# Two 128x512 products of a recurrence move from GpSimd to VectorE

## The chip, the cores and the metric

The kernel runs on one core of one Trainium2 chip. It computes one layer of a decoder trunk for 512 tokens. The metric is device time in microseconds (us). Three runs of the kernel before took 846.41, 846.49 and 846.69 us; their median is 846.49 us.

A core has a matrix engine (TensorE, PE in the profile; its weight loads are listed as PEld), a vector engine (VectorE, DVE), an activation engine (ScalarE, ACT), a general engine (GpSimd, POOL), and a queue that issues most transfers (SyncE, SP). Each engine takes its own instructions strictly in the order in which the kernel issued them to it. They wait for one another through semaphores.

## The reference, cut to what matters

The layer is a half-step feed-forward block, a token mixer, and a second half-step feed-forward block. The change lies in the mixer. There a gated linear recurrence on 512 channels stands beside a sliding-window attention with 8 heads:

```python
r = jax.nn.sigmoid(block_diag(xc, w_rg, b_rg))
i = jax.nn.sigmoid(block_diag(xc, w_ig, b_ig))
log_a = LRU_C * r * jax.nn.log_sigmoid(lam)
a = jnp.exp(log_a)
mult = jnp.sqrt(-jnp.expm1(2.0 * log_a))
u = mult * (i * xc)                       # "inputs with their roots"
h = scan(h[t] = a[t] * h[t-1] + u[t])
y_lru = h * jax.nn.gelu(gate_lru)
p = softmax over (band of scores, sink)   # per block of 128 queries
y = concat(rms_norm(y_lru), rms_norm(p @ v)) @ w_o
```

The change concerns the product `mult * (i * xc)`.

## The kernel before, in words

Activations lie with channels on the 128 partitions and the 512 tokens along the free axis. The 512 recurrence channels are therefore four chunks, `ci` 0 to 3, each a 128x512 float32 tile. `us_[ci]` holds `i * xc` (in the profile this tile is named `xc`), `th[ci]` holds what becomes the root, and `rs_[ci]` the decay `a` (named `r`).

The order of all instructions is written out by hand; no planner moves anything. The mixer's middle part is a loop over `now` from 0 to 9 (line 1706). It drives eight attention units, `units[0]` to `units[7]`: four blocks of 128 queries (`b`) times two key/value groups (`n`). Each unit passes through four steps, spread over three turns of the loop:

- `scores` (lines 1618 to 1632): PE's score products for a block, issued once per block; then on DVE the mask (`COPY_PREDICATED`), a maximum (`TENSOR_REDUCE`), the negated maximum `nm` (L1630) and the sink's exponent `es` (L1632).
- `exps` (lines 1641 to 1645): four exponentials on ACT, which need `nm`; then the denominators on POOL (`den`, L1645).
- `turn_p`, one turn later (lines 1653 to 1660): PE transposes the probabilities (`pt`, L1653), ACT copies them out (`pa`, L1655), and POOL makes the part of the previous block (`pp`, L1659) and of the current one (`pa`, L1660) with two affine selects.
- `values`, two turns later (lines 1672 to 1680): PE multiplies with the values (`po`; L1672 needs `pp`, L1673 needs `pa`), and after every second unit DVE normalises (`yn`, L1680).

Between these steps `pump` issues pieces of the gate's projection on PE (`gt`, lines 498 to 500, three matmuls a piece), so that PE has work while the other engines prepare its next operands. `PUMPS` says how many pieces stand at each place. PE runs through this list in order too: if a transpose or a value product is not ready, the gate pieces behind it wait.

The recurrence is woven into the same loop. In turn 5 ACT takes the four square roots (L1573). In turn 6, behind unit 6's `scores` and other DVE work, stand the four products `root_u` (L1576) and the scans of chunks 2 and 3 (L1581). Unit 7's `scores` are behind those on DVE. On POOL, `root_u` stands behind unit 5's affine selects and unit 6's `den`, and ahead of unit 6's affine selects. Chunk 0's scan follows in turn 8 and chunk 1's behind the loop; a deferred split of an output weight (L184) follows chunk 0's scan on DVE. Behind the loop 5 pieces of the gate's projection are left for PE, then the transposes `atp` (L1751), then the output projection `wo` (L1794 and on).

## Time and profile before

| what | value |
|---|---|
| median of three runs | 846.49 us (846.41 to 846.69) |
| the profiled execution's own time | 847.31 us |
| its span, first to last instruction | 845.6 us |
| PE busy | 835.3 us, 99% of the span |
| DVE busy | 734.1 us, 87% |
| ACT busy | 525.1 us, 62% |
| POOL busy | 202.1 us, 24% |
| mean granted TensorE clock | 0.999 |

The timeline's columns are start (us from the span's start), duration in us, engine, line, operation, tiles as out<-in, shapes, and the count of instructions merged into the row. Brackets at the end give the engine's idle time in front of the row and what ended it. The duration of a row counts from when the instruction is issued to its engine, so it contains time in which it is held up there. Neighbouring instructions of one engine overlap by a little under 0.1 us, so the next row's start tells when an engine is free again. In the view of waits each row names who waited for whom, with the total in us, the count, and the longest single wait.

### The profile page before, as it was taken

Reading aid. Unit: us, or ns where it says so; the run is one execution under the profiler, and the core shown is the slowest. Engines: PE = TensorE matmul, PEld = TensorE weight load, DVE = VectorE, ACT = ScalarE, POOL = GpSimd, SP = SyncE. Lnnn points to the kernel's source line nnn. Section 1 sums busy time; section 2 is a strip of 40 time slices with the busy share of each in tenths; the row PEclk is TensorE's granted clock in tenths of the full one; section 3 lists DMA queues with packets and bytes.
Section 4 is the critical chain, followed back from the end, with each engine's and each line's share of the span. In section 5 each row is a group of like instructions: output and inputs, shape, how many; then the busy total and the mean of one; then the engine's idle time right before and its main releaser. Section 6 shows DMA issues by size and latency. Waiting matters only on the chain.

```text
span 845.6 us, 12586 instructions
## 1 busy us (share of the span) xinstructions
PE 835.3 (99%) x4568; PEld 725.1 (86%) x4568; DVE 734.1 (87%) x1020; ACT 525.1 (62%) x875; POOL 202.1 (24%) x213
## 2 busy tenths in 40 slices
PE   9999999999999999999999999999999999999996
PEld 9988888988988998998788899888788888888885
DVE  4978999988979865889989589799998998998996
ACT  6746756676666655556888447436657767666562
POOL 2023000230320334334456055112004114032001
PEclk9999999999999999999999999999999999999999
DMA  7249419397594899231311130167639939769742
GB/s 250 76 141 348 158 47 320 84 246 251 140 253 169 178 274 322 74 101 50 101 50 51 50 121 31 50 167 190 231 110 230 319 89 250 256 152 259 297 138 101
DMA packets 122767, 142.18 MB, mean 168 GB/s; under 512 B 23680, under 2 KB 81360, under 8 KB 122192
## 3 DMA queue, kind: packets, MB, share of 16 engines
q1 hardware_dynamic: 108576, 110.81, 40.8%
q0 software_dynamic: 13984, 30.42, 16.8%
q8 instruction: 36, 0.59, 0.3%
q14 instruction: 27, 0.22, 0.1%
q10 hardware_dynamic: 144, 0.13, 0.0%
HBM read 100.45 MB, written 40.89 MB: 167 GB/s over the span
## 4 chain that ended last, share of the span: by engine, by line
PE 89%; DVE 5%; DMA 2%; ACT 2%; issue 1%; POOL 1%; SPq 0%; DVEq 0%; ACTq 0%; POOLq 0%
PE aa L948 10%; PE ab L948 10%; PE da L948 5%; PE db L948 5%; PE yaa L1339 3%; PE bb L948 3%; PE ba L948 3%; PE yda L1339 2%; PE ya L498 2%; PE ya L499 2%; PE ya L500 2%; PE aa L878 1%; PE a_first L1198 1%; PE yab L1865 1%; PE yab L1863 1%; PE yab L1864 1%
## 5 line engine op out<-in xcount | busy, mean ns | idle before, releaser
L1108 POOL DMA_DIRECT2D yp_a<-stage x42 | 36.8, 1067 | 181.7 <-ACT stage L1105 160.9
L1108 POOL DMA_DIRECT2D yp_b<-stage x42 | 36.3, 1032 | 144.9 <-ACT stage L1105 121.6
L498 PE MATMUL ya<-hha,whi_ad 128*128 128x512 f32 x62 | 24.1, 389 | 0.0
L499 PE MATMUL ya<-hla,whi_ad 128*128 128x512 f32 x62 | 24.1, 389 | 0.0
L500 PE MATMUL ya<-hha,wlo_ad 128*128 128x512 f32 x62 | 24.1, 389 | 0.0
L681 POOL TENSOR_TENSOR acca_r<-acca_r,sq_r 128x512 f32<-128x512 f32 x6 | 8.0, 1326 | 45.4 <-ACT sq_r L529 45.4
L1977 POOL TENSOR_TENSOR last<-yp,grow 128x512 f32<-128x512 f32 x3 | 3.9, 1293 | 58.3 <-DVE yp L1972 58.3
L517 PE MATMUL an<-xh_mx,whi_xl 128*128 128x256 f32 x64 | 15.8, 287 | 0.0
L518 PE MATMUL an<-xh_mx,wlo_xl 128*128 128x256 f32 x64 | 15.5, 283 | 0.0
L1973 ACT ACTIVATE ysq<-yp 128x512 f32<-128x512 f32 (+1 forms) x9 | 5.3, 585 | 15.9 <-DVE yp L1972 15.7
L498 PE MATMUL gt<-xh_mx,whi_gt 128*128 128x512 f32 x32 | 14.2, 444 | 0.0
L500 PEld LDWEIGHTS ya<-hha,wlo_ad 128*128 128x128 f32 x62 | 11.6, 188 | 2.4
L1105 ACT COPY stage<-yab 128x512 f32<-128x512 f32 x12 | 6.5, 601 | 11.6 <-DMA yp_b<-stage 11.6
L498 PEld LDWEIGHTS ya<-hha,whi_ad 128*128 128x128 f32 x62 | 11.6, 188 | 2.4
L499 PEld LDWEIGHTS ya<-hla,whi_ad 128*128 128x128 f32 x62 | 11.6, 188 | 2.4
L529 ACT ACTIVATE sq_r<-yp_a 128x256 f32<-128x256 f32 (+1 forms) x10 | 5.0, 502 | 12.4 <-DVE yp_a L671 5.3
L498 PE MATMUL pub<-xh_f,whi_bu 128*128 128x512 f32 x32 | 12.6, 395 | 0.0
L500 PE MATMUL gt<-xh_mx,wlo_gt 128*128 128x512 f32 x32 | 12.6, 394 | 0.0
L498 PE MATMUL pgb<-xh_f,whi_bg 128*128 128x512 f32 x32 | 12.6, 393 | 0.0
L499 PE MATMUL gt<-xl_mx,whi_gt 128*128 128x512 f32 x32 | 12.6, 392 | 0.0
L498 PE MATMUL pq<-xh_mx,whi_q 128*128 128x512 f32 x32 | 12.5, 392 | 0.0
L573 ACT ACTIVATE xh_f<-xT,cols 128x256 fp32r<-128x256 f32 x16 | 8.1, 508 | 7.0 <-DVE xT L712 6.4
(2021 smaller groups left out, 3531.4 us busy)
## 6 DMA issues: line engine op xcount, KB each, us to landing
yp_a<-stage POOLq DMA_DIRECT2D x50, 256.0 KB, 8.9
yp_b<-stage POOLq DMA_DIRECT2D x50, 256.0 KB, 10.1
h_a<-za SPq DMA_DIRECT2D x16, 256.0 KB, 4.5
hxa<-h_a SPq DMA_DIRECT2D x16, 256.0 KB, 17.9
h_b<-zb SPq DMA_DIRECT2D x16, 256.0 KB, 3.7
hxb<-h_b SPq DMA_DIRECT2D x16, 256.0 KB, 18.8
xn<-in_x SPq DMA_DIRECT2D x8, 256.0 KB, 4.6
xT_hbm<-xT POOLq DMA_DIRECT2D x2, 1024.0 KB, 9.6
```

The lines of the kernel that those rows point to most:

```text
L498: pe.matmul(ps, hi[:, k, :], xh, start=start, stop=False)
L499: pe.matmul(ps, hi[:, k, :], xl, start=False, stop=False)
L500: pe.matmul(ps, lo[:, k, :], xh, start=False, stop=stop)
L517: pe.matmul(ps[:, sl], hi[:, k, :], xh, start=k == 0, stop=False)
L518: pe.matmul(ps[:, sl], lo[:, k, :], xh, start=False, stop=False)
L878: pe.matmul(o, w[:, k, js], x, start=first and i + j + k == 0, stop=k == 3 and i == 2, skip_group_check=True)
L948: pe.matmul(b[tb], x[:, blk], w[:, k, :], start=first and q + k + j == 0, stop=q + k == 2 and j == 2, skip_group_check=True)
L1108: pool.dma_start(o, st.rearrange("p (a b) -> p a b", a=2) if len(o.shape) == 3 else st, accum_op=ALU.add)
L1198: pe.matmul(banks[j][:, HALF[0]], ws[j][part][:, k, :], n1.xs[k][xpart][:, HALF[0]], start=k == 0 and part == xpart, stop=stop and k == KD ...
L1339: pe.matmul(o, a[:, k, ms], x[:, js], start=first and i + k + m % 2 == 0, stop=k == 1 and i == 2, skip_group_check=True)
L1863: pe.matmul(banks[i], hh[:, js], hi[:, k, :], start=first and k == 0, stop=False, skip_group_check=True)
L1864: pe.matmul(banks[i], hh[:, js], lo[:, k, :], start=False, stop=False, skip_group_check=True)
```

## The change

All four products are now issued to DVE. Chunks 0 and 1 were issued to POOL before. Nothing else is edited.

```diff
     def root_u(ci):
-        (pool if ci < 2 else dve).tensor_mul(us_[ci], us_[ci], th[ci])
+        dve.tensor_mul(us_[ci], us_[ci], th[ci])
```

The loop that calls it is unchanged, so on DVE the order becomes: products 0, 1, 2, 3, scans of chunks 2 and 3, then unit 7's scores. On POOL unit 6's affine selects follow directly behind its `den`. The scan of chunk 0 no longer waits for POOL. PE, ACT and SP have the same instructions in the same order; no transfer moves.

## The prediction

> **What bounds the kernel now.** I read the page's list of engines and its chain first. PE is busy all through, and the chain of work that ended last runs on PE for 89% of the span. A change elsewhere counts only where it makes PE wait, or ends a wait of PE.

> ```profile
> PE 835.3 (99%) x4568; PEld 725.1 (86%) x4568; DVE 734.1 (87%) x1020; ACT 525.1 (62%) x875; POOL 202.1 (24%) x213
> ...
> PE 89%; DVE 5%; DMA 2%; ACT 2%; issue 1%; POOL 1%; SPq 0%; DVEq 0%; ACTq 0%; POOLq 0%
> ```

> Next, the waits of PE alone. Apart from one at the start there are only these three:

> ```profile
> PE ab L948 <- ACT bb L953: 1.3, 1, 1.3
> PE yeb L1865 <- DVE hls L831: 0.3, 1, 0.3
> PE po L1673 <- POOL pa L1660: 0.3, 1, 0.3
> ```

> The last one is in our stretch: the value products of unit 6 wait for an affine select of POOL. So I read that stretch of the timeline engine by engine. POOL first:

> ```profile
> 441.67 1.47 POOL L1659 TENSOR_SCALAR_AFFINE_SELECT pp<-pa 128x512 f32<-128x512 f32 x1 [5.80 <-ACT pa L1655]
> 443.20 1.44 POOL L1660 TENSOR_SCALAR_AFFINE_SELECT pa<-pa 128x512 f32<-128x512 f32 x1
> 444.61 0.20 POOL L1645 TENSOR_TENSOR den<-dsum,es 128x4 f32<-128x4 f32 x1
> 444.76 2.51 POOL L1576 TENSOR_TENSOR xc<-xc,th 128x512 f32<-128x512 f32 x2
> 447.22 1.17 POOL L1659 TENSOR_SCALAR_AFFINE_SELECT pp<-pa 128x512 f32<-128x512 f32 x1
> 448.46 0.64 POOL L1660 TENSOR_SCALAR_AFFINE_SELECT pa<-pa 128x512 f32<-128x512 f32 x1
> 449.06 0.20 POOL L1645 TENSOR_TENSOR den<-dsum,es 128x4 f32<-128x4 f32 x1
> 449.21 0.64 POOL L1659 TENSOR_SCALAR_AFFINE_SELECT pp<-pa 128x512 f32<-128x512 f32 x1
> 449.91 1.44 POOL L1660 TENSOR_SCALAR_AFFINE_SELECT pa<-pa 128x512 f32<-128x512 f32 x1
> ```

> The two products occupy POOL from 444.76 to 447.27, and unit 6's selects (447.22, 448.46) stand behind them. An affine select takes 0.64 us alone and about 1.45 in company. DVE in the same stretch:

> ```profile
> 440.28 1.28 DVE L1576 TENSOR_TENSOR xc<-xc,th 128x512 f32<-128x512 f32 x2
> 441.48 2.72 DVE L1581 TENSOR_TENSOR_SCAN xc<-r,xc 128x512 f32<-128x512 f32 x2
> 444.13 0.40 DVE L1626 COPY_PREDICATED sc<-up,sc 128x256 f32<-128x256 uint8 x1
> ...
> 445.82 0.22 DVE L1630 SCALAR_TENSOR_TENSOR nm<-mx,nsink 128x4 f32<-128x4 f32 x1
> 446.08 1.22 DVE L1632 TENSOR_TENSOR es<-nm,sinks 128x4 f32<-128x4 f32 x1
> ...
> 449.30 1.61 DVE L1581 TENSOR_TENSOR_SCAN xc<-r,xc 128x512 f32<-128x512 f32 x1
> 450.84 1.58 DVE L184 TENSOR_TENSOR wlo_wo<-raw_wo__4318,whi_wo 128x1024 fp32r<-128x1024 f32 x1
> ```

> DVE has no idle time from 440.28 to 450.84: products 2 and 3, two scans, unit 7's scores from 444.13. The 128x4 operation at 446.08 takes 1.22 us and ends at 447.30, just when POOL's product ends (447.27). [...]

> ```profile
> L1581 DVE TENSOR_TENSOR_SCAN xc<-r,xc x4: 1217/1404/1614, 441.5 to 455.9; 128x512 f32<-128x512 f32 x4
> ```

> Last, ACT and PE. ACT's first exponential of unit 7 waits for DVE's `nm`, so ACT has no slack there. PE's gate piece at 447.78 stands behind the transposes of those exponentials.

> ```profile
> 445.04 0.61 ACT L1655 COPY pa<-pt 128x512 f32<-128x512 f32 x1
> 446.14 0.37 ACT L1641 ACTIVATE sc<-sc,nm 128x128 f32<-128x128 f32 x1 [0.49 <-DVE nm L1630]
> ...
> 448.06 0.59 ACT L1655 COPY pa<-pt 128x512 f32<-128x512 f32 x1 [0.32 <-PE pt L1653]
> ```

> ```profile
> 447.05 0.97 PE L1653 MATMUL pt<-ident,sc 128*128 128x128 f32 x4
> 447.78 0.48 PE L498 MATMUL gt<-xh_mx,whi_gt 128*128 128x512 f32 x1
> ...
> 448.57 0.33 PE L1672 MATMUL po<-home,pp 128*128 128x64 f32 x2
> 449.15 0.43 PE L1673 MATMUL po<-home,pa 128*128 128x64 f32 x2 [0.25 <-POOL pa L1660]
> ...
> 450.73 0.48 PE L498 MATMUL gt<-xh_mx,whi_gt 128*128 128x512 f32 x1
> ...
> 451.52 0.33 PE L1672 MATMUL po<-home,pp 128*128 128x64 f32 x2
> ...
> 453.22 0.47 PE L498 MATMUL gt<-xh_mx,whi_gt 128*128 128x512 f32 x1
> ```

> **The change, step by step.** Two products leave POOL and two enter DVE. No instruction of PE, ACT or SP moves, and no transfer is issued elsewhere.

> Step 1, the added products on DVE. Two products start at 440.28 and the next instruction at 441.48, so one costs 0.60 us and two more cost 1.20. DVE has no idle time behind them to take that up, so unit 7's scores come at least 1.20 later. The roots are ready: products 2 and 3, whose roots are the last, already run at 440.28.

> Step 2, hold-ups between DVE and POOL. Unit 5's selects start at 441.67 whatever DVE does (ACT's copy releases them). Before, they met the two scans. The scans took 2.65 us from start to the next start (441.48 to 444.13) where twice 1.22 is 2.44, so some 0.2 to 0.3 was lost: one hold-up, because the second select ended (444.64) after the scans. After, the first select comes during product 2, the second during product 3, and each is let in between two DVE operations. That is two hold-ups. One costs DVE 0.39 (1.61 minus 1.22), so I add one more, 0.4. Bounds: nothing, if the second select again slips behind all DVE work, and 0.8, if unit 6's `den` makes a third hold-up. I take the middle, since both selects ask while a DVE operation runs and another follows.

> [...]

> Step 3, what waits for it. Unit 7's scores start at 444.13 + 1.20 + 0.40 = 445.73, and `nm` is 1.6 later. ACT's exponentials start at 446.14 + 1.6 = 447.74. PE resumes its gate piece 1.64 after the first exponential now (446.14 to 447.78), so then at 449.38 in place of 447.78. PE loses 1.6 us; it arrives at the transposes no later than now and stands there. Bounds 1.2 and 2.0 from step 2.

> Step 4, the gain on POOL. Without the products unit 6's selects need only ACT's copy (445.04 + 0.61 = 445.65) and a gap behind the last scan; at 0.64 to 0.8 each they end near 447.1. PE arrives at unit 6's values at 449.38 + 0.79 = 450.17 and finds them done. Now these take 2.16 us (448.57 to 450.73) against 1.70 of unit 7's (451.52 to 453.22). So PE gets back 0.46. It can't be more, because only this wait of PE lies on POOL. PE is now 1.14 late.

> Step 5, unit 7's selects, which stand behind the late transposes. PE wants them at 450.17 + 1.70 + 0.79 = 452.66, the current block's part 0.16 later, at 452.82. ACT's copy runs at 448.06 + 1.6 = 449.66 and ends at 450.25. DVE, meanwhile, gets `es` (446.08) without the wait for POOL's product, so its lag falls from 1.6 to about 0.6 and chunk 0's scan starts at about 449.9. The first select asks at 450.3 during that scan, is let in at its end near 451.0 and ends at 451.6. The second meets the split L184, which starts at 451.0, is held up by 0.39, takes 1.58 and ends near 452.5; the select then ends near 453.05. PE waits about 0.25. Bounds: 0, if the select goes ahead of the split, and 0.7, if both selects come behind it. PE's lag is 1.14 + 0.25 = 1.4.

> Step 6, further on. The rows above show PE without slack behind 453.22, and the mixer's norms and the second feed-forward block all start from what PE makes; I add nothing. Chunk 0's scan and the split end near 452.5 and DVE must next have `yn`, which waits for PE's values in both kernels, so it is not late by more than PE.

> Sum: 1.6 - 0.46 + 0.25 = +1.4 us. On the profiled execution's 847.31 that is 848.7; on the median, 0.82 below that execution, 846.49 + 1.4 = **847.9 us**, or 0.17% more. The ends of the steps give 1.2 - 0.46 + 0 = +0.7 and 2.0 - 0.46 + 0.7 = +2.2, so 847.2 to 848.7.

> **The rivals.** Clearly slower by bigger hold-ups. The place is unit 5's and unit 7's selects; the price is a whole select, 0.64, for each of two hold-ups, so 1.28 in step 2 less the 0.25 lost now, which is 1.0 in place of 0.4, and PE stands 2.2 long. With the wait of step 5 that is 2.2 - 0.46 + 0.25 = +2.0, with 0.7 there +2.4: 848.5 to 848.9. It decides when unit 7's scores start later than about 446.0. For it speaks the 1.22 us that a 128x4 operation lost; against it, the scan's 0.39. [...]

> Absorbed later. PE's 1.3 us wait for ACT's `bb` in the second feed-forward block could shrink by what PE comes late, if what it waits for does not hang on PE. Then 846.49 + 1.4 - 1.3 = 846.6. It needs transfers or DVE work there to start independently of the mixer's end; I see none, since they work on the mixer's output.

> Not slower at all: the products were a piece of what PE waited for, and the added work on VectorE hides beside the attention. Then only step 4 acts: 846.49 - 0.46 = 846.0. It decides when `nm` is no later than 446.14. Against it speaks that DVE has no idle time there and ACT waits 0.49 for it.

> **How the numbers follow.** The forecast has 0.55, bigger hold-ups 0.27, absorbed later 0.12, not slower 0.06. A change under 0.2%, 1.7 us, is about what a measurement of this kernel can tell from none. The forecast's own range, 847.2 to 848.7, crosses the bound at 848.18; I give 0.20 of its 0.55 to the far side. With 0.25 of the bigger hold-ups, slower has 0.45. Faster by over 0.2% would need more than all of PE's wait here and I give it 0.03, half of the last rival's. The rest, 0.52, is within. The range takes in part of the absorbed case and the bigger hold-ups: 846.5 to 849.0.

> **What would show it.** In the profile after: four products on DVE in a row, unit 7's first mask near 445.7, ACT's wait for `nm` grown from 0.49 to about 2.1, PE's transposes at 447 followed by a gate piece near 449.4, no wait of PE for unit 6's select, and a short one for unit 7's. The 128x4 `es` should fall to about a tenth of a microsecond or two. Wrong would be: unit 7's mask at 445.3 or before (fewer hold-ups) or after 446.0 (bigger ones); PE's lag at 453 differing from the lag at the end (then something later takes it up or adds to it).

## The result, and the profile after

The changed kernel takes 853.91 us in the median of seven runs, the kernel before 846.54: a ratio of 1.0066, 95% interval 1.0049 to 1.0082. It is slower, by 0.66%, and its median lies outside the range that was given. The ratio is nearer to that of the means (1.0067) than to that of the medians (1.0087), since not all executions lost alike.

The seven times are not one group. Two are 848.51 and 848.59 us, with a mean granted TensorE clock of 0.998; five are 853.46 to 855.15 us, with 0.989 to 0.991. The first profile happened to be of a short execution (848.51 us). It shows what the change does to the waits, and so it is read first. Its page, in the lines that answer to those of before:

```profile
PE 836.0 (99%) x4568; PEld 725.3 (86%) x4568; DVE 733.8 (87%) x1022; ACT 524.5 (62%) x875; POOL 198.7 (23%) x211
...
PE 94%; DVE 3%; ACT 1%; POOL 0%; issue 0%; DMA 0%; SPq 0%; DVEq 0%; ACTq 0%; POOLq 0%
```

All waits of PE in the same execution:

```profile
PE warm L1185 <- POOL ident masks.py:199: 1.4, 1, 1.4
PE pt L1653 <- ACT sc L1641: 1.2, 1, 1.2
PE ab L948 <- ACT bb L953: 0.6, 1, 0.6
PE yeb L1865 <- DVE hls L831: 0.3, 1, 0.3
PE po L1673 <- POOL pa L1660: 0.2, 1, 0.2
```

A new wait has come, 1.2 us for unit 7's exponentials at the transposes. The wait for GpSimd is still there with 0.2 us, but it is now unit 7's. DVE's timeline shows where the new wait is from:

```profile
440.51 2.92 DVE L1576 TENSOR_TENSOR xc<-xc,th 128x512 f32<-128x512 f32 x4
443.36 2.76 DVE L1581 TENSOR_TENSOR_SCAN xc<-r,xc 128x512 f32<-128x512 f32 x2
446.04 0.40 DVE L1626 COPY_PREDICATED sc<-up,sc 128x256 f32<-128x256 uint8 x1
...
447.73 0.16 DVE L1630 SCALAR_TENSOR_TENSOR nm<-mx,nsink 128x4 f32<-128x4 f32 x1
447.92 0.16 DVE L1632 TENSOR_TENSOR es<-nm,sinks 128x4 f32<-128x4 f32 x1
```

Four products in a row, the two scans, and only then unit 7's scores, at 446.04 in place of 444.13. The 128x4 operation takes 0.16 us where it took 1.22. On POOL, unit 6's selects follow ACT's copy at once and end at 447.28:

```profile
441.89 1.00 POOL L1659 TENSOR_SCALAR_AFFINE_SELECT pp<-pa 128x512 f32<-128x512 f32 x1 [5.80 <-ACT pa L1655]
442.96 0.97 POOL L1660 TENSOR_SCALAR_AFFINE_SELECT pa<-pa 128x512 f32<-128x512 f32 x1
443.90 1.10 POOL L1645 TENSOR_TENSOR den<-dsum,es 128x4 f32<-128x4 f32 x1
445.94 0.63 POOL L1659 TENSOR_SCALAR_AFFINE_SELECT pp<-pa 128x512 f32<-128x512 f32 x1 [0.94 <-ACT pa L1655]
446.64 0.63 POOL L1660 TENSOR_SCALAR_AFFINE_SELECT pa<-pa 128x512 f32<-128x512 f32 x1
```

PE's timeline shows the hole. After 447.3 PE has four transposes at 0.35 us from start to start, each as soon as its exponential is there, and nothing else until 449.62:

```profile
446.86 0.40 PE L500 MATMUL gt<-xh_mx,wlo_gt 128*128 128x512 f32 x1
448.50 1.37 PE L1653 MATMUL pt<-ident,sc 128*128 128x128 f32 x4 [1.24 <-ACT sc L1641]
449.62 0.48 PE L498 MATMUL gt<-xh_mx,whi_gt 128*128 128x512 f32 x1
...
452.11 0.47 PE L498 MATMUL gt<-xh_mx,whi_gt 128*128 128x512 f32 x1
...
454.95 0.47 PE L498 MATMUL gt<-xh_mx,whi_gt 128*128 128x512 f32 x1
```

In this execution the span is 1.2 us longer than the profiled one of before (845.6 to 846.8), which was itself 0.8 above its median; the two short executions are 2.0 us above that median. So the waits in the mixer are close to the forecast, and they are not what makes the median 7 us longer. The theory from this profile, called A: in most executions the hole makes the granted clock fall for some us. The rival, B: the time of the long executions is lost at another place, or by another engine.

### The profile page after: what moved, and what is told of

Same layout as the page of the kernel before. It is cut to its first block, busy times and chain, and to the rows that moved or that the text cites. A ratio compares the mean times of both kernels' runs of the same rounds, so it can differ in the third digit from the quotient of the medians.

```text
span 846.8 us, 12586 instructions
## 1 busy us (share of the span) xinstructions
PE 836.0 (99%) x4568; PEld 725.3 (86%) x4568; DVE 733.8 (87%) x1022; ACT 524.5 (62%) x875; POOL 198.7 (23%) x211
## 4 chain that ended last, share of the span: by engine, by line
PE 94%; DVE 3%; ACT 1%; POOL 0%; issue 0%; DMA 0%; SPq 0%; DVEq 0%; ACTq 0%; POOLq 0%
PE aa L948 10%; PE ab L948 10%; PE da L948 5%; PE db L948 4%; PE yaa L1339 3%; PE bb L948 3%; PE ba L948 3%; PE yda L1339 2%; PE ya L499 2%; PE ya L498 2%; PE ya L500 2%; PE aa L878 1%; PE a_first L1198 1%; PE yab L1864 1%; PE yab L1863 1%; PE yab L1865 1%
## 5 line engine op out<-in xcount | busy, mean ns | idle before, releaser
L498 PE MATMUL ya<-hha,whi_ad 128*128 128x512 f32 x62 | 24.1, 389 | 0.0
L498 PE MATMUL gt<-xh_mx,whi_gt 128*128 128x512 f32 x32 | 14.2, 444 | 0.0
L498 PEld LDWEIGHTS ya<-hha,whi_ad 128*128 128x128 f32 x62 | 11.6, 188 | 2.4
L498 PE MATMUL pub<-xh_f,whi_bu 128*128 128x512 f32 x32 | 12.7, 395 | 0.0
L498 PE MATMUL pgb<-xh_f,whi_bg 128*128 128x512 f32 x32 | 12.6, 393 | 0.0
L498 PE MATMUL pq<-xh_mx,whi_q 128*128 128x512 f32 x32 | 12.6, 393 | 0.0
L500 PE MATMUL pq<-xh_mx,wlo_q 128*128 128x512 f32 x32 | 12.5, 390 | 0.0
```

Of the source, the lines that this page charges most:

```text
L498: pe.matmul(ps, hi[:, k, :], xh, start=start, stop=False)
L500: pe.matmul(ps, lo[:, k, :], xh, start=False, stop=stop)
```

## The experiments

**The changed kernel once more, unedited,** to get a profile of a long execution.

> The changed kernel once more, unedited. Its executions fell into two groups: about 848.5 us at a mean granted TensorE clock of 0.998, and 853.5 to 855.2 us at 0.989 to 0.991. Theory A (the clock): PE's wait for unit 7's exponentials, grown to 1.24 us with four widely spaced transposes behind it, lets the granted clock fall for some us in most executions, so a profile of a long execution shows the clock below 1.00 directly behind about 448 us, matmuls there at a start-to-start of more than 0.23 us, and some 5 us lost there. Theory B (lost elsewhere): the clock is low, or the time lost, at another place, such as the second feed-forward block's wait for ACT's bb near 598 us, and the stretch behind 448 us is as in the profile at hand.

It took 853.65 us beside 847.04 of the kernel before (ratio 1.0067, 1.0050 to 1.0084). Of ten executions eight are at 852.79 to 854.79 us with a clock of 0.990 to 0.992, two at 848.75 and 848.99 with 0.999. The executions of the kernel before that ran beside it have 0.997 or more, all of them. The profiled one is long, 853.10. Its busy time in two stretches (length, then PE, PEld, DVE, ACT, POOL, then the granted clock):

```profile
447.54:450.96 3.42, 2.28 (x12) 1.59 (x12) 3.26 (x8) 2.53 (x11) 0.47 (x2) 1.00 0.00 0
450.96:461.20 10.24, 10.24 (x40) 9.30 (x39) 4.28 (x9) 5.12 (x12) 4.87 (x4) 0.50 0.29 102
```

From 450.96 to 461.20, just behind the hole, the clock is at half. The timeline of PE around the edge shows the pairs of value products going from 0.22 to 0.43 us:

```profile
450.69 0.39 PE L1673 MATMUL po<-home,pa 128*128 128x64 f32 x2
450.92 0.59 PE L1672 MATMUL po<-home,pp 128*128 128x64 f32 x2
451.29 0.63 PE L1673 MATMUL po<-home,pa 128*128 128x64 f32 x2
451.72 0.63 PE L1672 MATMUL po<-home,pp 128*128 128x64 f32 x2
```

By estimate from that row, 10.24 us at 0.50 cost up to 5.1 us. The span is 851.4 us, 4.6 longer than that of the short execution, whose waits are nearly the same (1.2 us at the transposes in both, 0.7 and 0.6 for `bb`). That is the missing time, and it lies where theory A has it.

**The delay without the change of engine.** GpSimd keeps its two products; VectorE gets two operations of the same size that change no value.

```diff
         if now == 6:
+            for ci in (2, 3):
+                dve.tensor_tensor(th[ci], th[ci], th[ci], op=ALU.max)
             for ci in range(KC):
                 root_u(ci)
```

> The kernel before, with GpSimd keeping its two products, and two more 128x512 operations on VectorE ahead of its products (a maximum of a root with itself, which changes no value). So VectorE has the delay of the change while the two products do not change engine. Theory A: PE's wait at unit 7's transposes is as long as in the changed kernel (1.2 us or more) and long executions appear with a clock near 0.99, some 853 us; the others are at 848 to 849. Theory B: no long group, at most 849 us.

It took 855.32 us beside 847.04 (ratio 1.0097, 1.0082 to 1.0112). All four executions have a clock of 0.989 or 0.990; the short ones that were expected did not occur. PE's wait is longer than in the changed kernel, and the clock is at half for longer:

```profile
PE pt L1653 <- ACT sc L1641: 1.8, 1, 1.8
```

```profile
446.66:450.07 3.41, 1.62 (x10) 0.99 (x8) 3.27 (x8) 0.80 (x5) 3.34 (x4) 1.00 0.00 0
450.07:463.73 13.66, 13.64 (x50) 12.01 (x50) 6.91 (x13) 7.07 (x19) 6.37 (x6) 0.50 0.23 77
```

So VectorE's delay ahead of unit 7's scores is enough. The products need not leave GpSimd for it.

**The hole filled, the delay left.** Five 128x512 matmuls whose result is overwritten stand ahead of unit 7's transposes of the changed kernel. The layer's output does not depend on them.

```diff
         pt = bank(f"pt{b}{n}")
+        if (b, n) == (NB - 1, 1):
+            for _ in range(5):
+                pe.matmul(pt, mx.xs[0][0][:, :P], mx.xs[0][0], start=True, stop=True)
```

> The changed kernel with five 128x512 matmuls more on PE ahead of unit 7's transposes, into the bank that the transposes then overwrite. They change no wait for data: the exponentials are as late as before, and five matmuls at 0.23 us fill 1.14 us of PE's 1.24 us of waiting. Theory A (the clock falls because PE does too little in this stretch): the clock stays at 1.00, and although PE has more work all executions are in the short group, 848.2 to 849.0 us, so some 5 us faster than the changed kernel. Theory B (the late exponentials cost the time by themselves, or through other engines): most executions at 853 us or more.

It took 848.65 us beside 846.94 (ratio 1.0022, 1.0012 to 1.0032); all eight clocks are 0.997 to 0.999. Seven executions are at 848.08 to 849.39 us, close to what was expected; one is at 850.55, well above it, with a wait of 1.8 us for `bb`. The exponentials are as late as in the changed kernel, which this PE timeline shows (the transposes moved to L1656):

```profile
447.74 1.32 PE L1653 MATMUL pt<-xh_mx 128*128 128x512 f32 x5
449.14 1.38 PE L1656 MATMUL pt<-ident,sc 128*128 128x128 f32 x4
450.27 0.48 PE L498 MATMUL gt<-xh_mx,whi_gt 128*128 128x512 f32 x1
```

More work made the kernel faster, 1.0022 against 1.0067. This separates the two parts of the loss, averaged over the executions: some 0.2% is PE's lag, some 0.45% is the clock. Theory B falls.

**The hole made smaller.** One of the five gate pieces left behind the loop goes ahead of the transposes.

```diff
-PUMPS = [(2, 1)] * 8 + [(1, 1), (1, 0), (4, 0)]
+PUMPS = [(2, 1)] * 8 + [(2, 1), (1, 0), (4, 0)]
```

> The changed kernel with one of the five gate pieces that are left behind the loop issued ahead of unit 7's transposes. PE's wait there shrinks by one piece, 0.7 us, from 1.24 to about 0.55; up to 0.5 us of waiting may appear at the attention's last transposes, which have one piece less ahead of them. The sum of waits is about the same. Theory A: the single wait is short enough in most or all executions, the clock stays near 0.998 and the time is 848 to 848.8 us. Theory B: long executions as often as in the changed kernel.

It took 848.50 us beside 847.04 (ratio 1.0017, 1.0007 to 1.0026), all ten executions at 848.10 to 849.14 with clocks of 0.997 to 0.999. The wait at the transposes is 0.5 us. Two others have come, 0.2 at the attention's last transposes and 0.4 in the second feed-forward block (`stage`), so that PE's waits behind the start sum to 2.2 us where the short execution of the changed kernel has 2.3. With about the same sum, none of ten executions lost the clock at a single wait of 0.5 us, where eight of ten executions of the changed kernel, with one of 1.2, had 0.990 to 0.992: here it goes with the single hole, and not with the sum of the waits.

**Half the change:** three products on VectorE, one on GpSimd.

```diff
-        dve.tensor_mul(us_[ci], us_[ci], th[ci])
+        (pool if ci < 1 else dve).tensor_mul(us_[ci], us_[ci], th[ci])
```

> Half the change: three products on VectorE, one on GpSimd. VectorE's delay falls by one product, 0.6 us, and PE's wait at unit 7's transposes from 1.24 to about 0.6 us. Theory A: the clock stays at 1.00 in all or nearly all executions, and the time is 0.4 to 1.2 us above the kernel before, so half the change costs far less than half of the 6 to 7 us. Theory B (the loss grows with the delay): about half of the loss, 3 us or more.

It took 848.88 us beside 846.94 (ratio 1.0024, 1.0013 to 1.0035). Its median is 1.9 us above the kernel before where I had 0.4 to 1.2 for theory A. In the mixer the wait at the transposes is halved, but the wait for GpSimd is not 0.2 us as in the changed kernel but 0.6:

```profile
PE ab L948 <- ACT bb L953: 1.9, 1, 1.9
...
PE pt L1653 <- ACT sc L1641: 0.6, 1, 0.6
PE po L1673 <- POOL pa L1660: 0.6, 1, 0.6
```

But the clock holds through the mixer: six of seven executions have 0.997 to 0.999. The seventh, the profiled one (0.995, 851.18 us), lost it at another place, behind the wait of 1.9 us for `bb` in the second feed-forward block, for one short stretch:

```profile
602.00:606.00 4.00, 4.00 (x12) 3.10 (x11) 3.97 (x4) 4.00 (x6) 0.00 (x0) 0.57 0.02 4
```

So here the clock fell (a mean of 0.57 over 4 us) behind another wait than that for the exponentials. It need not: in the profiled execution of the filled kernel PE waited 1.8 us for `bb` and the clock held at 1.00. Half the change costs a third of the loss, though its executions lag about as much as the short ones of the whole change. What it lacks is the fall of the clock in the mixer, which fits a loss that comes in a step.

**Another order on VectorE.** All four products stay on VectorE, but they and the two scans stand behind unit 7's scores.

```diff
             scores(*units[now])
+            if now == 7:
+                for ci in range(KC):
+                    root_u(ci)
+                for ci in (2, 3):
+                    scan(ci)
...
-        if now == 6:
-            for ci in range(KC):
-                root_u(ci)
-            for ci in (2, 3):
-                scan(ci)
```

> All four products stay on VectorE, but they and the two scans stand behind unit 7's scores instead of ahead of them. The wait of ACT for nm (2.1 us) and PE's wait at the transposes (1.24 us) should go. Theory A: no execution is in the long group, all have a clock near 0.998, and with unit 6's wait for GpSimd gone too the time is 845.7 to 846.5 us. Theory B (the products' engine itself, or something later, is what makes the long executions): 853 us in most executions, as for the changed kernel.

It took 846.29 us beside 847.04 (ratio 0.9994, 0.9984 to 1.0003), with no long execution in ten. All waits of PE:

```profile
PE warm L1185 <- POOL ident masks.py:199: 1.4, 1, 1.4
PE yeb L1865 <- DVE hls L831: 0.3, 1, 0.3
PE ab L948 <- ACT bb L953: 0.3, 1, 0.3
```

The wait at the transposes is gone. With the same products on the same engine the loss of the change has vanished, so it hangs on the order. The interval holds 1, and the same kernel ran again in more executions:

> The kernel with all four products on VectorE and unit 7's scores ahead of them once more, with more rounds. The first time it took 846.29 us where the kernel before took 847.04, but the interval of the ratio, 0.9984 to 1.0003, holds 1. If its gain is PE's wait of 0.25 us for the affine select and the 0.2 to 0.4 us around unit 7's transposes, the ratio is 0.9990 to 0.9995 and the interval may end just below 1. If the first result was chance, the ratio is within 0.0003 of 1. In neither case is an execution longer than 848.5 us.

846.59 us beside 847.00 (ratio 0.9995, 0.9986 to 1.0004), no execution above 847.63. Twice some 0.05% faster than the kernel before, and twice not clear of no change: whether it beats the kernel before stays open. It clearly beats the changed one.

**The same order with the products' engines of the kernel before,** two on GpSimd and two on VectorE:

> Unit 7's scores ahead of the products and scans, with the products' engines as in the kernel before (two on GpSimd, two on VectorE). If only the order on VectorE matters, the time is that of the other kernel with scores first, 0.5 to 1.0 us below the kernel before. If the products' engine matters too, through unit 6's affine selects on GpSimd, PE's wait for them stays at 0.3 us or more and the time is 0.2 to 0.6 us above the other kernel with scores first. In both cases no long executions.

It took 850.51 us beside 846.94 (ratio 1.0048, 1.0024 to 1.0072), which neither expectation had. Three of six executions are long, 852.32 to 853.48 us at 0.991 or 0.992; three are 847.05 to 848.70 at 0.997 or 0.998. PE waits in another place:

```profile
PE po L1672 <- POOL pp L1659: 0.9, 1, 0.9
PE po L1673 <- POOL pa L1660: 0.6, 1, 0.6
```

In this order GpSimd's two products run beside VectorE's two scans and they hold each other up: the products take 3.89 us (2.51 before) and the scans 4.46 (2.72 before). Unit 6's selects behind the products end at 450.06, where they ended at 449.10 before. So the engine matters after all: behind the scores, VectorE is the better place for all four products; ahead of them it is better to leave two on GpSimd. And half of the executions have a low clock, though the profiled one, a short one, has no wait for the exponentials. Where the long ones lose the clock is not shown, since none of them was profiled; the waits for GpSimd's selects are the likely place. That no execution would be long was my mistake here: I had looked only at the wait that the order removes.

## Why the prediction was right and wrong

Measured in the short execution, less the 0.23 us by which DVE was already late at its first product (440.51 against 440.28):

- Steps 1 and 2, the delay of unit 7's scores: forecast 1.60, measured 1.68 (446.04 against 444.13, less 0.23). The two more products and one more hold-up are right, at 1.2 and 0.5. The hold-ups came one operation later than forecast: the fourth product took 1.12 us in place of 0.68, the first scan 1.65 in place of 1.22. The 0.2 to 0.3 that the prediction read off the two scans of before is too little, since it left out the overlap of neighbours: a free scan takes 1.13 from start to start (450.10 to 451.23 in the short execution), so the two lost 0.39, a whole hold-up.
- Step 3, PE's resumption behind the transposes: forecast 1.6 late, measured 1.61 (449.62 against 447.78). ACT's wait for `nm` is 2.1 us as forecast.
- Step 4, the gain on GpSimd: right. PE's lag falls to 1.15 (452.11 against 450.73), forecast 1.14.
- Step 5, unit 7's selects: forecast 0.25 us of waiting and 1.4 of lag, measured 1.50 of lag (454.95 against 453.22).
- Step 6, nothing further on: wrong. In the profiled long execution the clock is at half for 10.24 us.

The wait for `bb` is shorter in the short execution (0.6 us) than in the profiled one of before (1.3), but the traces speak against reading this as the rival "absorbed later". ACT's copy for `bb` stands behind a cast that waits for VectorE, and in the profiled execution of before VectorE waited there for a weight transfer:

```profile
DVE raw_bx__6121 L294 <- DMA raw_by__6246<-in_ffn_w_gu: 1.1, 1, 1.1
```

This wait comes and goes with the execution. It is missing in the short one of the changed kernel, but 1.2 us in the filled kernel and 1.4 with three products, whose PE is late as well; there the wait for `bb` is 1.8 and 1.9. Where VectorE does not wait for the transfer, the wait for `bb` is 0.7 us or less, whether PE is late or not. The long execution comes 4.6 us later than the short one and still waits 0.7.

The step that failed is what step 3 made of its own number. Its "PE loses 1.6 us" was priced by the length of the wait alone, and step 6 added nothing for what a wait does to the work behind it. The runs show a price of its own for the hole: in 13 of 17 executions of the changed kernel the mean granted clock is 0.989 to 0.992, these are some 5 us longer than the others, and in the one of them that was profiled the clock falls right behind the hole. The four short executions, 848.51 to 848.99, are inside the range; the median is not. None of the rivals had the clock. The bigger hold-ups, to which I gave the chance of being slower, did not occur. Their price for one, a whole select of 0.64 us, is shown by no run: the two hold-ups cost 0.44 and 0.43 us, about the 0.39 that step 2 took. That each select is let in between two operations of VectorE was an estimate too; what the rows show is those two losses, and unit 5's selects at 1.00 and 0.97 us in place of 1.47 and 1.44. The forecast's +1.4 us had the right sign, and the size was off by a factor of five. The case that had the largest chance, a change under 0.2% (0.52), did not come.

The trace of before shows no fall of the clock while PE had work (1.00 in each stretch read up to 800 us), and its own holes are shorter. But its rows allowed the question: the hole that step 3 worked out, from the end of one gate piece to the next, is 2.4 us long with four small transposes in it. The longest wait in that trace behind its start is the 1.3 us for `bb`, without such a tail, and it kept the clock (1.00 from 596 to 604). So no row could vouch for the clock behind the longer hole, and the range should have said so.

## What to carry to other kernels

Price a wait of TensorE twice: by its length, and by what the clock may do behind it; here one of 1.2 us went with some 5 us more in 13 of 17 executions. Where a change makes one hole with little work in it, here of 2.4 us, look at the mean granted clock of every execution, since a single profile can be of one that kept it. Where the delay can't be avoided, splitting the hole or filling it with matmuls of no use can cost less than losing the clock, as it did here (ratios of 1.0017 and 1.0022 against 1.0067); better still, put what the matrix engine waits for ahead of what can wait.

## What the runs showed of the hardware

The rows below are of stretches of 3.41 us, counted on from 7.2 us into the span, where PE's `warm` matmuls go from 3 to 6 in 0.4 us (6.80 to 7.20 and 7.20 to 7.60 in the short execution of the changed kernel). That these are the stretches to compare was my guess. They lie almost alike in the short and the long execution of the changed kernel; the long one has 0.09 us less of PE's work in the stretch with the hole. First the short one:

```profile
447.51:450.92 3.41, 2.37 (x13) 1.67 (x13) 3.25 (x8) 2.61 (x12) 0.56 (x2) 1.00 0.00 0
```

PE is busy for 2.37 us of it and the clock stays at 1.00 (450 to 452); in the long one it was 2.28 and the clock fell to 0.50, in the kernel with two more operations 1.62, with the same fall. The smaller hole and the filled one left 2.82 and 3.26, and the clock stayed at 1.00:

```profile
445.95:449.36 3.41, 2.82 (x15) 1.83 (x14) 3.18 (x10) 1.33 (x8) 1.27 (x2) 1.00 0.00 0
```

```profile
447.15:450.56 3.41, 3.26 (x14) 1.99 (x13) 3.22 (x9) 1.60 (x10) 0.91 (x3) 1.00 0.00 0
597.34:600.75 3.41, 2.25 (x10) 1.52 (x9) 3.17 (x3) 1.86 (x2) 0.00 (x0) 1.00 1.04 417
```

The last row, of the second feed-forward block in the same execution, has 2.25 us and kept its clock (1.00 from 602 to 606). With three products the stretch ahead of the fall has 1.46 us. The stretch in which PE's work ends, in the profiled execution with the scores first, has 1.83, and the clock stays at 1.00 for 3.41 us more, in which PE does nothing:

```profile
598.79:602.20 3.41, 1.46 (x7) 0.92 (x6) 3.41 (x4) 3.41 (x5) 0.00 (x0) 1.00 0.66 264
```

```profile
835.51:838.92 3.41, 1.83 (x16) 1.63 (x14) 3.04 (x9) 1.83 (x7) 0.00 (x0) 1.00 0.40 154
838.92:842.33 3.41, 0.00 (x0) 0.00 (x0) 1.71 (x4) 0.20 (x1) 0.00 (x0) 1.00 0.37 137
842.33:843.90 1.57, 0.00 (x0) 0.00 (x0) 0.00 (x0) 0.00 (x0) 0.00 (x0) 0.50 0.12 41
```

So 1.83 and 2.25 kept the clock where 2.28 lost it, and PE's busy time in such a stretch does not tell by itself which hole loses the clock. What does, these runs don't settle.

A small thing beside it. A 128x4 operation of GpSimd (`den` at 443.90) took 1.10 us, where the next (449.66) took 0.20, while VectorE's scan ran (443.36 on), and VectorE's 128x4 `es` took 1.22 us before and 0.16 after. So hold-ups showed on both of these engines, and these two small operations took over five times as long in one.
